# Sharing the last copies of a linear-attention kernel with VectorE, and filling TensorE's waits with products nobody reads

## The chip, the cores and the metric

One core of one Trainium2 chip. The metric is the device time in microseconds (us) of one execution of the whole kernel; each kernel was executed several times, and medians and ranges are given. The profiler's span (first to last instruction, 124.9 us for the kernel before) is some 1.8 us shorter than the time (126.69 us for the same execution).

## The reference, cut to what matters

```python
# Q, K, V: float32 [8, 12, 512, 64]
Q_feat = np.maximum(0, Q); K_feat = np.maximum(0, K)
KV     = einsum('bhkd,bhkv->bhdv', K_feat, V)
K_sum  = sum(K_feat, axis=2)
out    = einsum('bhqd,bhdv->bhqv', Q_feat, KV) / (einsum('bhqd,bhd->bhq', Q_feat, K_sum)[..., None] + 1e-10)
```

96 heads are done in 12 octets of eight. Every byte is read once (37.75 MB) and written once (12.58 MB).

## The kernel before: the parts that matter

An octet (number `o`) passes through these steps: K and V are prepared on VectorE (`prep`), KV is summed on TensorE into one PSUM bank (`mm_kv`), copied to SBUF (`evac_kv`), Q is transposed on TensorE and copied with a ReLU (`qt`), the outputs are made on TensorE and copied (`out_t`), the denominators are made (`denom`), the outputs are transposed back (`back`), divided on VectorE (`norm`) and stored (`store`).

```python
    pou = pool("pou", 2, space=PSUM)            # two buffers, shared by out_t and back
    ps_kv = pkv.tile([P, 2, 256], fp32)         # one PSUM bank for KV
    def evac_kv(o, gs):                         # four copies for half an octet
        for s in range(2):
            for c in range(2):
                nc.scalar.copy(kvd[o % NK][...], ps_kv[64 * s:64 * s + 64, gs, ...])
    def qt(o):                                  # two halves; of the last octet VectorE takes the second
        ...
    def out_t(o):
        for j in range(2):
            ps = pou.tile(..., tag="ps_out")
            ...                                 # 4 products of 256 columns
            copy = nc.vector.tensor_copy if o == NO - 1 and j == 1 else nc.scalar.copy
            copy(ot[o][:, :, 4 * j:4 * j + 4], ps.rearrange(...))
    def store(o, o_sb):
        if o + DELAY < NO:                      # DELAY = 5: hold stores back until later loads have landed
            nc.sync.dma_start(out=scratch, in_=k_sb[2 * (o + DELAY)][0:1, 0, :])
        if o == NO - 1:                         # the last octet in two halves
            for j in range(2): nc.sync.dma_start(out=Ov[:, rs], in_=o_sb[:, rs])
            return
        nc.sync.dma_start(out=Ov, in_=o_sb)     # 1 MB
    def backs(o):
        o_sb = out_tile()
        for j in range(2):
            norm(o, j, back(o, j), o_sb)
        store(o, o_sb)
    ...
    o = NO - 2; g = 2 * NO - 2                  # the last two octets
    ...
    prep(g + 1); prep_v(g + 1, nc.vector)
    backs(o)
    mm_kv(g + 1)
    evac_kv(o + 1, slice(1, 2))
    qt(o + 1)
    out_t(o + 1)
    denom(o + 1)
    backs(o + 1)
```

## Time and profile before

| | before |
|---|---|
| time, first three executions | 126.67 us (126.56 to 126.73) |
| busiest compute engine | PE, 69% of the span |
| HBM traffic over the span | 403 GB/s |
| last normalising round ends | 121.37 us into the span |
| first and second half store issued | 119.88 and 121.40 |
| last mark of the last store, slowest DMA engine | 123.65 |

Two lines of the timeline (start, duration, engine, line and what it does; SPq is SyncE's queue of DMA issues) give the moments at which the last three stores are handed over:

```profile
113.02 0.33 SPq L236 DMA_DIRECT2D out_dram<-o_sb  x1
...
119.88 1.85 SPq L234 DMA_DIRECT2D out_dram<-o_sb  x2
```

The first is the last full store, of octet 10, the second line the two halves of octet 11 (119.88 and 121.40). Here a store that is issued starts only when the DMA engines have done what was issued before it (octet 10's, issued at 113.02, gets its first packets at about 117.0).

### The profile page before, as it was taken

Reading aid. Unit: us, or ns where it says so; the run is one execution under the profiler, and the core shown is the slowest. Engines: PE = TensorE matmul, PEld = TensorE weight load, DVE = VectorE, ACT = ScalarE, POOL = GpSimd, SP = SyncE. Lnnn points to the kernel's source line nnn. Section 1 sums busy time; section 2 is a strip of 40 time slices with the busy share of each in tenths; the row PEclk is TensorE's granted clock in tenths of the full one; section 3 lists DMA queues with packets and bytes.
Section 4 is the critical chain, followed back from the end, with each engine's and each line's share of the span. In section 5 each row is a group of like instructions: output and inputs, shape, how many; then the busy total and the mean of one; then the engine's idle time right before and its main releaser. Section 6 shows DMA issues by size and latency. Waiting matters only on the chain.

```text
span 124.9 us, 2637 instructions
## 1 busy us (share of the span) xinstructions
PE 86.0 (69%) x1056; PEld 78.7 (63%) x1056; DVE 81.6 (65%) x175; ACT 78.9 (63%) x115; POOL 31.3 (25%) x62
## 2 busy tenths in 40 slices
PE   0032297998989899894598596199867757795640
PEld 0041285997878789793597494199756566694630
DVE  2256644749798897979348759532946936994670
ACT  0163369969898998989339589164929928647000
POOL 6902424315253331142133124034022000000000
PEclk9999999999999999999859999657999999999687
DMA  3999999999999999999999999999999999999984
GB/s 102 380 310 214 215 207 210 217 205 214 207 212 211 208 217 326 255 216 297 286 213 284 304 211 252 332 212 234 339 226 217 323 259 216 314 425 420 428 352 197
DMA packets 10748, 32.68 MB, mean 262 GB/s; under 512 B 1392, under 2 KB 1392, under 8 KB 9328
## 3 DMA queue, kind: packets, MB, share of 16 engines
q0 software_dynamic: 8064, 17.83, 74.6%
q1 hardware_dynamic: 2384, 13.63, 27.2%
q10 hardware_dynamic: 288, 1.05, 2.1%
q8 instruction: 8, 0.13, 0.4%
q14 instruction: 4, 0.03, 0.1%
HBM read 37.75 MB, written 12.58 MB: 403 GB/s over the span
## 4 chain that ended last, share of the span: by engine, by line
DMA 34%; PE 28%; DVE 26%; ACT 6%; issue 2%; SPq 0%; DVEq 0%; ACTq 0%; POOLq 0%
DMA v_sb<-in_V_dram 14%; DMA q_sb<-in_Q_dram 13%; DVE o_sb L221 12%; PE ps_kv L148 11%; PE ps_bk L215 8%; DMA kv_first<-in_K_dram 7%; PE ps_qt L171 5%; DVE kf L134 4%; ACT qt L176 4%; PE ps_ot L187 3%; ACT kvd L157 2%; DVE vo L136 2%; DVE vo L143 2%; DVE den L205 1%; DVE rec L209 1%
## 5 line engine op out<-in xcount | busy, mean ns | idle before, releaser
L148 PE MATMUL ps_kv<-vo,kf 128*128 128x132 bf16 x384 | 31.0, 246 | 17.9 <-ACT vo L141 8.2
L148 PEld LDWEIGHTS <-kf 128*128 128x128 bf16 x384 | 28.5, 110 | 19.2 <-DVE vo L136 10.9
L221 DVE TENSOR_TENSOR o_sb<-ps_bk,rec 128x1024 f32<-128x1024 f32 x24 | 28.4, 1220 | 16.7 <-PE ps_bk L215 16.7
L157 ACT CAST kvd<-ps_kv 64x260 bf16<-64x260 f32 (+1 forms) x56 | 19.2, 342 | 18.8 <-PE ps_kv L148 16.1
L176 ACT ACTIVATE qt<-ps_qt 128x1024 bf16<-128x1024 bf16 x23 | 22.4, 1026 | 6.7 <-PE ps_qt L171 6.6
L215 PE MATMUL ps_bk<-ident,ot_sb 128*128 128x128 f32 x192 | 24.5, 284 | 1.1 <-DVE ot_sb L190 1.1
L190 ACT COPY ot_sb<-ps_ot 128x1024 f32<-128x1024 f32 x23 | 23.0, 1013 | 2.9 <-PE ps_ot L187 2.0
L134 DVE TENSOR_SCALAR kf<-k_sb,mask 128x1024 bf16<-128x1024 bf16 x44 | 18.3, 457 | 7.5 <-DMA k_sb<-in_K_dram 7.5
L215 PEld LDWEIGHTS ps_bk<-ident,ot_sb 128*128 128x128 f32 x192 | 22.4, 149 | 1.1 <-ACT ot_sb L190 1.1
L92 POOL DMA_DIRECT2D k_sb<-in_K_dram x22 | 11.9, 542 | 37.9 <-DMA q_sb<-in_Q_dram 20.6
L171 PE MATMUL ps_qt<-ident,q_sb 128*128 128x128 bf16 x192 | 15.2, 243 | 7.2 <-DMA q_sb<-in_Q_dram 7.2
L171 PEld LDWEIGHTS <-q_sb 128*128 128x128 bf16 x192 | 13.7, 110 | 8.2 <-DMA q_sb<-in_Q_dram 8.0
L187 PE MATMUL ps_ot<-qt,kvd 128*128 128x256 bf16 x96 | 14.5, 283 | 5.6 <-DVE o_sb L221 4.3
L94 POOL DMA_DIRECT2D v_sb<-in_V_dram x22 | 12.4, 562 | 17.5 <-DMA k_sb<-in_K_dram 9.5
L187 PEld LDWEIGHTS <-kvd 128*128 128x128 bf16 x96 | 9.3, 100 | 8.2 <-issue 6.1
L136 DVE TENSOR_SCALAR vo<-v_sb,mask 128x1024 bf16<-128x1024 bf16 x22 | 10.7, 488 | 1.5 <-DMA v_sb<-in_V_dram 1.5
L141 ACT ACTIVATE vo<-v_sb,mask 128x1024 bf16<-128x1024 bf16 x10 | 11.5, 1154 | 0.2
L197 PEld LDWEIGHTS <-qt 128*128 128x128 bf16 x192 | 6.8, 97 | 4.4 <-ACT qt L176 3.4
L197 PE MATMUL ps_den<-kvd,qt 128*128 128x16 bf16 x192 | 7.5, 180 | 2.4 <-ACT qt L176 2.1
L98 POOL DMA_DIRECT2D q_sb<-in_Q_dram x12 | 6.5, 544 | 8.2 <-DMA v_sb<-in_V_dram 5.3
L200 DVE SCALAR_TENSOR_TENSOR own<-ps_den,mask_h 128x256 f32<-128x256 f32 x12 | 5.0, 416 | 3.3 <-PE ps_den L197 3.3
L134 DVE TENSOR_SCALAR kf<-kv_first,mask 128x1024 bf16<-128x1024 f32 x4 | 2.8, 751 | 5.1 <-DMA kv_first<-in_K_dram 5.1
(22 smaller groups left out, 26.4 us busy)
## 6 DMA issues: line engine op xcount, KB each, us to landing
out_dram<-o_sb SPq DMA_DIRECT2D x11, 1024.0 KB, 9.1
q_sb<-in_Q_dram POOLq DMA_DIRECT2D x12, 512.0 KB, 14.7
k_sb<-in_K_dram POOLq DMA_DIRECT2D x22, 256.0 KB, 14.1
v_sb<-in_V_dram POOLq DMA_DIRECT2D x22, 256.0 KB, 13.2
kv_first<-in_V_dram ACTq DMA_DIRECT2D x2, 512.0 KB, 7.3
kv_first<-in_K_dram SPq DMA_DIRECT2D x2, 512.0 KB, 6.9
out_dram<-o_sb SPq DMA_DIRECT2D x2, 512.0 KB, 2.7
scratch<-k_sb SPq DMA_DIRECT2D x7, 0.1 KB, 4.8
```

The costliest lines, as they stand in the source:

```text
L94: nc.gpsimd.dma_start(out=v_sb[g].rearrange("p r d -> p (r d)"), in_=Vr[g])
L134: nc.vector.tensor_scalar(kf[g][:, :, s, :], k_sb[g], scalar1=0.0, scalar2=mask[:, 0, s:s + 1], op0=Alu.max, op1=Alu.mult)
L136: nc.vector.tensor_scalar(vo[g % NB][:, :, 0, 2:D + 2], v_sb[g], scalar1=mask[:, 1, 0:1], scalar2=None, op0=Alu.mult)
L148: nc.tensor.matmul(ps_kv[:, g % 2, 0:2 * (D + 2)].rearrange("p (t d) -> p t d", t=2), kf[g][:, r, :, :].rearrange("p s d -> p (s d)"), vo[ ...
L157: nc.scalar.copy(kvd[o % NK][64 * c:64 * c + 64, 4 * gs.start + s:4 * gs.stop:2, c * D1:c * D1 + D1].rearrange("p (g t) d -> p g t d", t=2 ...
L171: nc.tensor.transpose(ps[:, u, :], q_sb[o][:, i * (U // 2) + u, :], ident)
L176: nc.scalar.activation(qt_sb[o % NZ][:, us], ps, Act.Relu)
L187: nc.tensor.matmul(ps[:, i], kvd[o % NK][:, h, 1:2 * D + 1], q[:, :, h, :], start=True, stop=True, skip_group_check=True)
L190: copy(ot[o][:, :, 4 * j:4 * j + 4], ps.rearrange("p h u c -> p u h c"))
L197: nc.tensor.matmul(ps[:, u], qt_sb[o % NZ][:, u, :], kvd[o % NK][:, :, 0:2 * D1:2 * D1 - 1], start=True, stop=True, skip_group_check=True)
L215: nc.tensor.transpose(ps[:, 2 * v:2 * v + 2].rearrange("p c d -> p (c d)"), ot[o][:, 8 * j + v].rearrange("p h c -> p (h c)"), ident32)
L221: nc.vector.tensor_tensor(o_sb[:, rs], ps, rec[o][:, rs].unsqueeze(2).to_broadcast([P, 16, D]), op=Alu.mult)
```

## The change

Its intent: in the last two octets ScalarE does most copies in a row while VectorE waits, and TensorE waits so long for them that its clock is halved. So VectorE takes two of KV's four copies and half of Q ahead of the second normalising round of octet 10, ScalarE takes both output copies of the last octet, and TensorE runs 5 and 6 products into an unread part of a PSUM bank, to look busy to the clock gate.

```diff
+    ps_den = pde.tile([P, 2, 256], fp32, name="ps_den")     # half for denominators, half for idle products
-    def evac_kv(o, gs):
+    def evac_kv(o, gs, share=False):
...
+                copy = nc.vector.tensor_copy if share and c == 1 else nc.scalar.copy
...
+    def idle(n, o):
+        for i in range(n):
+            nc.tensor.matmul(ps_den[:, 1], ident, q_sb[o][:, 2 * i:2 * i + 2, :], start=True, stop=True,
+                             skip_group_check=True)
...
-            copy = nc.vector.tensor_copy if o == NO - 1 and j == 1 else nc.scalar.copy
-            copy(ot[o][:, :, 4 * j:4 * j + 4], ps.rearrange("p h u c -> p u h c"))
+            nc.scalar.copy(ot[o][:, :, 4 * j:4 * j + 4], ps.rearrange("p h u c -> p u h c"))
...
-    backs(o)
+    o_sb = out_tile()
+    norm(o, 0, back(o, 0), o_sb)
+    ps = back(o, 1)
     mm_kv(g + 1)
-    evac_kv(o + 1, slice(1, 2))
-    qt(o + 1)
-    out_t(o + 1)
+    evac_kv(o + 1, slice(1, 2), share=True)
+    for i in range(2):
+        relu_q(o + 1, i, transp(o + 1, i), nc.vector if i == 1 else None)
+    norm(o, 1, ps, o_sb)
+    store(o, o_sb)
+    idle(5, o + 1)
+    out_t(o + 1, (0,))
     denom(o + 1)
+    out_t(o + 1, (1,))
+    idle(6, o + 1)
     backs(o + 1)
```

## The prediction

> **What bounds the kernel now.** I read the 40 slices first, for what is full all the time.
>
> ```profile
> PEclk9999999999999999999859999657999999999687
> DMA  3999999999999999999999999999999999999984
> ```
>
> Each digit is a slice of 3.12 us. The DMA row is 9 from the second slice to the third last: the 16 DMA engines are never short of work, while no compute engine is above 69% of the span. The PEclk row shows the second thing: the granted TensorE clock falls at slices 19 and 25 to 27, and again at the end (6, 8, 7). The change is aimed at that last fall, so the end decides. The second view is the chain that ended last, from 113 us on.
>
> ```profile
> 113.07 1.03 ACT qt L176
> 114.10 0.04 issue
> 114.14 1.05 PE ps_ot L187 x8
> ...
> 115.28 1.23 DVE ot_sb L190
> 116.51 0.14 issue
> 116.65 3.47 PE ps_bk L215 x16
> 120.12 0.02 issue
> 120.14 1.23 DVE o_sb L221
> ```
>
> By it the end is compute: Q's copy, the output products, their copy, 16 transposes in 3.47 us, and the last normalising round, which ends at 121.37. The same 16 transposes took 1.75 us in the same chain at 109.22, so the half clock costs 1.72 us here. But the chain stops at the last instruction and the span ends at 124.9; the rest is the last stores. So third, stretches of the end with DMA share and GB/s as the last two columns (the first figures are the stretch's length and PE, PEld, DVE, ACT and POOL busy, then PEclk).
>
> ```profile
> 108.00:119.00 11.00, 8.50 (x99) 8.20 (x99) 8.24 (x16) 4.98 (x11) 0.00 (x0) 0.88 1.01 418
> 119.00:120.00 1.00, 1.00 (x7) 0.86 (x5) 0.85 (x1) 0.00 (x0) 0.00 (x0) 0.61 0.89 377
> 120.00:121.00 1.00, 0.11 (x1) 0.00 (x0) 0.86 (x1) 0.00 (x0) 0.00 (x0) 1.00 0.64 262
> 121.00:122.00 1.00, 0.00 (x0) 0.00 (x0) 0.37 (x1) 0.00 (x0) 0.00 (x0) 1.00 0.99 406
> 122.00:123.00 1.00, 0.00 (x0) 0.00 (x0) 0.00 (x0) 0.00 (x0) 0.00 (x0) 1.00 0.84 336
> 123.00:124.00 1.00, 0.00 (x0) 0.00 (x0) 0.00 (x0) 0.00 (x0) 0.00 (x0) 0.60 0.50 201
> ```
>
> From 108 to 119 us the DMA engines move 418 GB/s at share 1.01, by then almost only output. What they move is a backlog: the store of the last but one octet is issued at 113.0 and lands 8.4 us later, though 1 MB at 418 GB/s is 2.5 us. The DMA issues say the same (size, then us to landing):
>
> ```profile
> out_dram<-o_sb SPq DMA_DIRECT2D x11, 1024.0 KB, 9.1
> out_dram<-o_sb SPq DMA_DIRECT2D x2, 512.0 KB, 2.7
> ```
>
> So two paths reach the end almost together: compute, whose last half is ready at 121.37, and the store queue. I therefore counted the trace's packets. The five last full stores run back to back from 107.2; their packets finish on the fastest DMA engine at 119.44 and on the slowest at 121.04. That slowest engine took 2.45 us for each of these stores (its marks are 111.22, 113.68, 116.13, 118.58, 121.04), went at once to the first half store (issued 119.88, done there at 122.28) and then to the second (issued 121.40, first packet 122.22, last mark 123.65). It was not idle at all before 122.28.
>
> **What the Trainium skill says.** "TensorE: Matmul & The Clock Gate", Part 1, states a gate on the matmul clock that falls to half after a quiet window of about 3.4 us, the windows running freely. This trace agrees in size: the half-clock stretch runs from 116.37 to 119.78, 3.41 us. Cut on that grid, the windows show how much PE work kept the clock (second figure is PE busy, PEclk is the third last):
>
> ```profile
> 68.58:72.00 3.42, 1.85 (x26) 1.55 (x26) 2.58 (x7) 2.15 (x3) 0.53 (x1) 1.00 1.05 303
> ...
> 75.41:78.82 3.41, 1.68 (x25) 1.16 (x23) 3.34 (x8) 3.16 (x3) 1.06 (x2) 1.00 1.07 278
> 78.82:82.24 3.42, 1.50 (x15) 1.50 (x16) 0.82 (x3) 0.36 (x1) 0.53 (x1) 0.50 1.06 292
> ...
> 112.96:116.37 3.41, 1.45 (x24) 1.35 (x24) 1.74 (x3) 2.12 (x3) 0.00 (x0) 1.00 1.00 418
> 116.37:119.78 3.41, 3.13 (x15) 3.16 (x16) 2.39 (x5) 0.00 (x0) 0.00 (x0) 0.50 1.00 423
> ```
>
> After 1.68 and 1.45 us of PE work in a window the clock fell; after 1.85 it stayed. "PSUM — Partial Sum Buffer", PSUM bank collisions raise a hardware error, says that two engines may not touch one bank and quadrant at once. KV sits in one bank, and in the compiled order VectorE's two copies wait for ScalarE and ScalarE's second for VectorE, so the four copies go in turn; the trace of before, with ScalarE alone, can't show it. "DMA: Bandwidth & Descriptors", Queues, rings and completion order, says that each DMA engine consumes a queue's descriptors in ring order. The trace agrees: stores finish in the order of issue, each about 2.45 us after the one before. The same page, Where 436 GB/s comes from, gives a ceiling of 435 GB/s; 418 measured leaves little.
>
> **The change part by part.** Everything up to 110.6 us is the same: in the compiled order the first 1,725 rows of TensorE do not differ, and no load is moved.
>
> 1. KV's second half. Before: four ScalarE copies, 111.95 to 113.05. Now two of the four are VectorE's. A VectorE pass over 1,024 columns from PSUM took 1.22 us, over 256 columns 0.42, so about 0.29 us (estimate) for 130 columns against ScalarE's 0.27. In turn, with about 0.05 us for each change of engine, that is 1.25 us: ScalarE is done with its part at 112.87, VectorE at 113.2. ScalarE's half of Q starts at 112.9 instead of 113.07: gain 0.17.
> 2. VectorE's half of Q, 0.69 us, now comes before the second normalising round of octet 10: 113.2 to 113.9. So both halves of Q are there at about 113.95, 0.2 earlier than 114.14. That round (1.22) slips from ending at 113.0 to about 115.15, and with it its 1 MB store.
> 3. Output products: the copy of the second half moves from VectorE to ScalarE, which does both in 2 x 1.02 us one after the other: 114.5 to 116.55. Before, the two ran side by side and ended at 116.51. Gain from 1 and 2 given back: the transposes start at about 116.6 against 116.65.
> 4. Denominators: VectorE is free for them from 115.15 instead of 116.42; they were never last.
> 5. Idle products: 5 and 6 of 256 columns. Eight such products took 1.03 us, so about 0.65 and 0.75 us of PE, in gaps where it waits. The window that had 1.45 us of PE work then has some 2.8, over 1.85 by far. I expect the clock to hold whatever the phase of the windows. The 16 transposes then take 1.75 instead of 3.47 us.
>
> Sum for compute: normalising rounds end at about 118.7 and 119.95 instead of 119.86 and 121.37, so the last half is ready 1.4 us earlier. That is 1.1% and would give 125.3 us if nothing stood behind it.
>
> The store queue does. The half stores would be issued at 118.7 and 120.0, but the slowest DMA engine is busy with the full stores to 121.04. It then needs 1.25 us for each half (122.28 less 121.04), so it ends at 121.04 + 2.5 = 123.54 instead of 123.65. Gain: 0.11 us. The faster engines end earlier, which doesn't matter, as a store has landed when its last engine has. The late store of octet 10 costs nothing: it is issued at about 115.2, and even the fastest engine takes up its packets only at about 117.
>
> **The rivals.** (a) Compute alone sets the end: 1.4 us off, 125.3. The chain view speaks for it; the backlog speaks against it. (b) The DMA engines share the end evenly: their idle share from 119 to 123 is 0.11 + 0.36 + 0.01 + 0.16 = 0.64 us, so at most 126.0. Against it: a store's packets are fixed to their engines. But in another execution the spread of 1.6 us may be smaller. (c) The clock falls all the same, or the copies in turn cost more than I think: the last round then ends as before or some 0.3 us later, 126.6 to 127.0. (d) The late store of octet 10 leaves DMA engines idle: it has nearly 2 us of slack, so I give it little.
>
> For the queue speaks also that the three times before lie within 0.17 us. If free-running windows moved the half clock between executions, a compute-bound end would move by up to 1.4 us.
>
> **Range and chances.** The slowest engine gives 126.67 - 0.11 = 126.56; a little weight on (b) brings it to **126.5 us**. Low end 126.0 from (b), high end 126.8 from (c). Over 2% faster needs 124.1, more than the whole compute gain: 0.01. Slower by 2% needs 129.2: 0.01. Within 2%: 0.98.
>
> **What would show it.** Right: PEclk 1.00 up to 120 us and L215's counterpart for the last octet at about 1.75 us; the last normalising round ending near 120.0; DMA share about 1 up to 122 without the dip to 0.64; the half stores' time to landing up from 2.7 to some 3.6 us or more; the last landing moved by 0.1 to 0.6 us only. Wrong: a last landing 1 us earlier (the queue was no bound), a clock that still falls, or KV's four copies at the same time. The prediction fails as a whole if the store backlog at 119 us is smaller, or larger, than in the trace of before.

## The result, and the profile after

The changed kernel took 126.73 us (median of six, 126.59 to 126.78), the kernel before beside it 126.70 (median of six, 126.46 to 127.23; three of the six are those of the table above). The ratio is 0.9996, with a 95% interval from 0.9976 to 1.0016: the same. Here and below a ratio is the mean time of one kernel's fast runs over that of the other's in the same rounds, so not quite the ratio of the medians quoted.

What the change was for did happen. The granted clock and the DMA share by slices, after:

```profile
PEclk9999999999999999999779859959999999999995
DMA  3999999999999999999999999999999999999993
```

The fall of the clock at slices 38 to 40 is gone (only the last slice, with no work left, shows a 5). The chain at the end, after:

```profile
111.24 0.28 ACT kvd L160
111.52 0.02 issue
111.54 0.30 DVE kvd L160
111.84 0.02 issue
111.86 0.28 ACT kvd L160
112.14 0.02 issue
112.17 0.30 DVE kvd L160
...
116.09 1.11 PE ps_bk L228 x8
117.19 0.02 issue
117.22 1.22 DVE o_sb L234
```

KV's copies go in turn between ScalarE and VectorE, as the order of waits had said. Eight transposes now release the first normalising round 1.13 us after they start (117.22 less 116.09), where before it took 1.98 (118.63 less 116.65). The second round ends at 119.57 instead of 121.37. In this execution everything at 110 us was already 0.71 us earlier (octet 10's first round started at 109.93 instead of 110.64), so 1.09 of these 1.80 us belong to the change. Then the stretches of the end, with the columns as in the prediction:

```profile
108.00:119.00 11.00, 8.90 (x108) 7.79 (x105) 8.49 (x16) 4.77 (x10) 0.00 (x0) 1.00 1.01 416
119.00:120.00 1.00, 0.00 (x0) 0.00 (x0) 0.57 (x1) 0.00 (x0) 0.00 (x0) 1.00 1.00 422
120.00:121.00 1.00, 0.00 (x0) 0.00 (x0) 0.00 (x0) 0.00 (x0) 0.00 (x0) 1.00 0.96 397
121.00:122.00 1.00, 0.00 (x0) 0.00 (x0) 0.00 (x0) 0.00 (x0) 0.00 (x0) 1.00 1.03 422
122.00:123.00 1.00, 0.00 (x0) 0.00 (x0) 0.00 (x0) 0.00 (x0) 0.00 (x0) 0.64 0.66 270
123.00:124.00 1.00, 0.00 (x0) 0.00 (x0) 0.00 (x0) 0.00 (x0) 0.00 (x0) 0.50 0.15 61
```

From 120 us on no engine computes any more, and the DMA engines are full up to 122: the dip to 0.64 between 120 and 121 is filled, and what filled it is missing at the end (0.66 and 0.15 instead of 0.84 and 0.50). The half stores wait in the queue, as their time to landing shows, up from 2.7 us:

```profile
out_dram<-o_sb SPq DMA_DIRECT2D x2, 512.0 KB, 4.3
```

Counted by packets, the slowest DMA engine finishes the last half at 123.57 after and 123.65 before. (A mark is the 4-byte packet that ends an engine's share of a store in the trace. The packed trace has no engine numbers; which packets belong to one engine is inferred from their times.) Before, all 16 engines end together, from 123.50 to 123.65, because the fast ones ran out of packets and waited for the hand-overs at 119.88 and 121.40; after, they end one by one from 121.84 on. So the gain of 1.8 us in compute, 1.09 of it by the change, became 0.09 us at the last mark (before rounding), and the spans differ by 0.1 us (124.8 and 124.9). The rest turned into waiting in the store queue.

### The profile page after: what moved, and what is told of

Read it like the earlier page. It is cut to its first block, busy times and chain, and to the rows that moved or that the text cites. A ratio compares the mean times of both kernels' runs of the same rounds, so it can differ in the third digit from the quotient of the medians.

```text
span 124.8 us, 2656 instructions
## 1 busy us (share of the span) xinstructions
PE 86.6 (69%) x1067; PEld 78.5 (63%) x1067; DVE 81.1 (65%) x176; ACT 79.4 (64%) x114; POOL 31.2 (25%) x62
## 4 chain that ended last, share of the span: by engine, by line
DMA 34%; DVE 30%; PE 23%; ACT 5%; issue 2%; DVEq 1%; SPq 0%; POOLq 0%; ACTq 0%
DMA v_sb<-in_V_dram 14%; DVE o_sb L234 13%; DMA q_sb<-in_Q_dram 13%; PE ps_kv L150 11%; DMA kv_first<-in_K_dram 7%; PE ps_bk L228 7%; DVE kf L136 5%; PE ps_qt L171 4%; DVE vo L138 3%; ACT kvd L160 2%; DVE vo L145 2%; PE ps_ot L201 2%; DVE den L218 2%; ACT qt L179 2%; DVE rec L222 1%
## 5 line engine op out<-in xcount | busy, mean ns | idle before, releaser
L160 ACT CAST kvd<-ps_kv 64x260 bf16<-64x260 f32 (+1 forms) x54 | 18.7, 346 | 19.5 <-PE ps_kv L150 16.6
L203 ACT COPY ot_sb<-ps_ot 128x1024 f32<-128x1024 f32 x24 | 24.0, 1014 | 3.0 <-PE ps_ot L201 2.0
L228 PE MATMUL ps_bk<-ident,ot_sb 128*128 128x128 f32 x192 | 23.0, 273 | 0.4 <-ACT ot_sb L203 0.4
L228 PEld LDWEIGHTS ps_bk<-ident,ot_sb 128*128 128x128 f32 x192 | 20.8, 141 | 0.7 <-ACT ot_sb L203 0.7
L171 PE MATMUL ps_qt<-ident,q_sb 128*128 128x128 bf16 x192 | 16.0, 250 | 6.0 <-DMA q_sb<-in_Q_dram 5.9
L171 PEld LDWEIGHTS <-q_sb 128*128 128x128 bf16 x192 | 14.3, 114 | 7.3 <-DMA q_sb<-in_Q_dram 7.1
```

The lines of the kernel that those rows point to most:

```text
L160: copy(kvd[o % NK][64 * c:64 * c + 64, 4 * gs.start + s:4 * gs.stop:2, c * D1:c * D1 + D1].rearrange("p (g t) d -> p g t d", t=2), ps_kv[6 ...
L171: nc.tensor.transpose(ps[:, u, :], q_sb[o][:, i * (U // 2) + u, :], ident)
L203: nc.scalar.copy(ot[o][:, :, 4 * j:4 * j + 4], ps.rearrange("p h u c -> p u h c"))
L228: nc.tensor.transpose(ps[:, 2 * v:2 * v + 2].rearrange("p c d -> p (c d)"), ot[o][:, 8 * j + v].rearrange("p h c -> p (h c)"), ident32)
```

## The experiments

All variants compute the reference's result, except the three that leave out a store, which are marked. "Store queue" is my theory: the slowest DMA engine, never idle, reaches the end of its work at about 123.6 us whatever compute does, as long as compute hands over the last halves in time.

### A queue that is 1 MB shorter, on the kernel before (wrong output on purpose)

```diff
-        nc.sync.dma_start(out=Ov, in_=o_sb)
+        if o != NO - 3:
+            nc.sync.dma_start(out=Ov, in_=o_sb)
```

> The kernel before, without the store of octet 9 (its 1 MB of output stays unwritten: wrong on purpose). Theory (store queue): before, the queue of full stores and the compute tail reach the end within 0.1 us of each other, so with 1 MB (2.45 us of queue) less the compute tail alone sets the end: half stores issued at about 119.9 and 121.4 as now, time 126.3 to 126.7 us, at most 0.4 us less than before. Rival 1 (all bytes count, the DMA engines bound the whole kernel and compute never does): 2.4 us less, 124.3 us.

Measured: 126.09 us median of six, but from 124.34 to 127.06, against 126.76 (126.59 to 127.07, eleven) of before. Three of the six count as slow because they are over 1.5% above the fastest; the fast three are 124.34, 125.04 and 125.91, and give the ratio 0.9867 (0.9825 to 0.9908). That rule cuts off the upper half of a wide spread, so this ratio flatters; the median of all six is 0.5% under before. The expectation (126.3 to 126.7) missed: I had counted on the half clock at the end of every execution. The profiled one (125.91) kept its clock there and had its last round done at 120.27. Its stretches 118 to 120 show the queue run dry:

```profile
118.00:119.00 1.00, 0.73 (x7) 0.49 (x5) 1.00 (x1) 0.00 (x0) 0.00 (x0) 1.00 0.14 57
119.00:120.00 1.00, 0.00 (x0) 0.00 (x0) 1.00 (x2) 0.00 (x0) 0.00 (x0) 1.00 0.03 12
```

What follows: the queue was there; without this megabyte the profiled execution had its last mark at 122.73 instead of 123.65, and there compute set the end. The fastest execution, 2.4 us under before (126.76 less 124.34), is what the rival (all bytes count) had said. It has no trace, so this run alone doesn't exclude the rival. With the queue shortened even the fast executions spread over 1.6 us, while the kernel before spread over 0.5: this suggests that a full queue hides a spread of compute.

### The same on the changed kernel (wrong output on purpose), and once more

> The changed kernel, without the store of octet 9 (wrong on purpose). Theory (store queue): the queue ends on its slowest engine near 118.6 instead of 121.07, so the 1.7 us that the clock saves in the transposes show: last round ends near 119.6 to 119.9, last packet about 2.25 us after the second issue, time 124.9 to 125.3 us, 1.2 to 1.6 us less than the kernel before without this store. Rival 1 (all bytes count): 124.3 us, equal to the kernel before without it. Rival 2 (the earlier compute end is worth nothing in any case, for instance a fixed end of the program): 126.6 us, equal to the kernel before without it.

Measured: 126.46 us (126.02 to 127.06, six), ratio 0.9983 (0.9955 to 1.0011). This missed clearly. In its profile compute and queue were as expected (second half issued at 119.66, 15 of the 16 DMA engines done at 122.08), but one engine ended at 122.91. Among its last packets lies an 8 KB fetch of the queue that the profile calls q14, instruction, at 121.63; two of the 4 KB packets that followed took 368 and 308 ns instead of about 160.

> The changed kernel without the store of octet 9 once more, because its first run missed the 124.9 to 125.3 us expected (126.46). In that run's profile the last halves were done on 15 DMA engines at 122.08 and on one at 122.91, behind an 8 KB instruction fetch of the runtime's queue that began at 121.63 among its packets. Theory (a late fetch on one engine): the profile shows again one engine 0.5 us or more behind the other fifteen with such a fetch among its last packets, and the time is 126.0 to 127.1 us. Rival (chance of that one execution): all sixteen engines end within 0.35 us of each other and the profiled time is 125.0 to 125.4 us.

Measured: 126.49 us (125.95 to 126.87, four), ratio 0.9995 (0.9963 to 1.0027), and the same picture: 15 engines done at 121.92, one at 122.74, with a fetch at 121.46 and again packets of 368 and 308 ns behind it. The DMA share from 121 to 125 us in 40 slices, and that queue's line:

```profile
DMA  8997999400010010000000000000000000000000
...
q14 instruction: 1, 0.01, 0.5%
```

The first eight digits are all engines, the single 1s behind them one engine that is late. "DMA: Bandwidth & Descriptors", Queues, rings and completion order, of the Trainium skill calls row 14 of the queues runtime-internal, refill among its tasks; the traces agree, as the kernel issues nothing on it. The fetch (0.31 us) and the two longer packets (0.21 and 0.15 more than usual) make 0.67 of the 0.8 us by which this engine is late. So without the fetch the two profiled executions would have taken some 125.1 to 125.5 us, an estimate from their times (126.13 and 125.95) less 0.67 to 0.83, near the 124.9 to 125.3 expected. Why the fetch falls between the last packets here, and before them (119.30) in the variant above, no run shows. The slower executions of both runs (126.79 to 127.06) have no trace; that part stays open, and with it why the median hardly moved.

### The copies alone, and the idle products alone

The changed kernel without `idle(5, ...)` and `idle(6, ...)`; and the kernel before with them (the calls alone; `idle` and its `ps_den` as in the change):

```diff
     qt(o + 1)
+    idle(5, o + 1)
     out_t(o + 1)
     denom(o + 1)
+    idle(6, o + 1)
     backs(o + 1)
```

> The changed kernel without its 11 idle products: only the moved copies remain. Theory: the clock falls to half again before the last transposes (16 of them in about 3.4 us instead of 1.75 to 1.97), the last normalising round ends 1.4 to 1.7 us later, near 121.3, and the half stores wait for it; the time stays within 0.2 us of both kernels, 126.6 to 126.9 us, as the queue ends at about the same time. Rival (the copies alone kept the gain, the clock is not what matters): the last round still ends near 119.7 and the clock stays full.

> The kernel before with the 5 and 6 idle products alone, copies as before. Theory: the clock holds, the 16 transposes take 1.75 to 2.0 us, the last normalising round ends near 119.8 as in the changed kernel, because the moved copies give nothing (their gain is given back by ScalarE's two output copies in turn); time 126.5 to 126.8 us, equal to both. Rival (the idle products delay what stands behind them on TensorE, or do not hold the clock): last round at 121.3 or later.

Measured: copies alone 126.86 us (126.67 to 127.36, four), ratio 1.0012 (0.9991 to 1.0033). Idle products alone 126.97 (126.64 to 128.17, four), ratio 1.0032 (0.9995 to 1.0069). Neither differs from before by the interval. The details missed in both, and the second's time its 126.5 to 126.8. In the profiled execution of the copies alone the clock did not fall before the last transposes, so that one execution could not show what the idle products are for. With the idle products alone it did fall, and the last transposes started late. Two lines of the timeline of the idle products alone show why (in brackets, idle time and what ended it):

```profile
115.54 0.41 DVE L206 SCALAR_TENSOR_TENSOR own<-ps_den,mask_h 128x256 f32<-128x256 f32 x1
...
116.01 1.44 PE L183 MATMUL ps_den<-q_sb,ident 128*128 128x256 bf16 x6 [1.30 <-DVE own L206]
```

The six products write the bank that the denominators' pass reads, and in the compiled order they wait for that pass. In the kernel before it stands behind VectorE's output copy (114.40 to 115.63). So products meant to fill a wait stood in front of the transposes until 117.24. In the changed kernel the output copy is ScalarE's and that pass comes at 114.31: the moved copies are what makes room for the second idle products. A variant of it with the six ahead of the denominators tests this (against the diff above):

```diff
     out_t(o + 1)
-    denom(o + 1)
     idle(6, o + 1)
+    denom(o + 1)
     backs(o + 1)
```

> The kernel before with the idle products alone, as in the earlier run, but the second six ahead of the denominators' products instead of behind them. In the earlier run these six waited 1.30 us for the denominators' first VectorE pass, which stands behind VectorE's output copy, and held the transposes up to 117.24. Theory: without that wait the transposes start as the second copy ends (about 4.8 us after the end of Q's transposes, as in before), the clock holds in most executions, time 126.5 to 126.8 us with none above 127.0. Rival (the idle products do not hold the clock without the moved copies): the clock falls in the profiled run and single runs go over 127.0 us.

Measured: 126.68 us (126.56 to 126.91, six), ratio 0.9991 (0.9969 to 1.0013), no execution above 127.0, and in the profile eight transposes in 1.08 us from 116.81, with the clock at full. One profile can't show that the idle products hold the clock: it also held in those of the copies alone and of the shortened queue on the kernel before, which have none. The mean granted clock for every execution says more. The profiles in which it fell under the last transposes have a mean of 0.929 to 0.938, those in which it held 0.940 or more. In all 46 executions with idle products that wait for nobody (the changed kernel, its variants with these products, and this one) the mean is 0.938 or more; under 0.938 are 31 of 40 executions of before and two of the four of the copies alone. This kernel's six, without any moved copy, have 0.941 to 0.952. So the idle products hold the clock, in most executions at least, where they wait for nobody; and again the time is the same.

### More work in front of the last stores

The first normalising round of the last octet is done again, once or three times, with the same values:

```diff
-            norm(o, j, back(o, j), o_sb)
+            ps = back(o, j)
+            norm(o, j, ps, o_sb)
+            if o == NO - 1 and j == 0:
+                for _ in range(1):        # or 3
+                    norm(o, j, ps, o_sb)
```

> The changed kernel with the first normalising round of the last octet done twice (the same values again, 1.22 us more of VectorE ahead of both half stores; results stay right). Theory (store queue): the halves were issued at 118.5 and 119.6, and the slowest DMA engine would take them up only at 121.07 and 122.3, so both have about 1.8 us to spare: time 126.6 to 126.8 us, within 0.15 us of the changed kernel. Rival (the last round sets the end): 1.2 us more, 127.9 us.

> The same with three more rounds, 3.66 us of VectorE ahead of both half stores. Theory: 1.8 us of it fall into the slack and the rest shows, 1.7 to 2.1 us more than the changed kernel, 128.4 to 128.8 us. Rival (the last round sets the end): 3.7 us more, 130.4 us. If the queue had more slack than the packets say: less than 1.5 us more.

> The kernel before with one more such round. Theory: here compute and queue ended within 0.1 us of each other where the clock had fallen, so in executions with the half clock at the end the 1.22 us show (127.7 to 128.0 us), in executions whose clock held they show in part or not at all; median of 127.0 to 127.9 us, clearly more than the changed kernel with the same round. Rival (both kernels end by the queue with the same slack): within 0.15 us of before.

| kernel | VectorE work added | time, us | ratio to before |
|---|---|---|---|
| changed, one round more | 1.22 us | 126.88 (126.54 to 127.16) | 1.0003 (0.9978 to 1.0028) |
| changed, three more | 3.66 us | 128.77 (128.70 to 129.11) | 1.0156 (1.0131 to 1.0181) |
| before, one more | 1.22 us | 127.09 (126.69 to 127.90) | 1.0030 (0.9997 to 1.0062) |

This is the clearest answer. 1.22 us straight in front of the last stores cost the changed kernel nothing that the interval (0.25%, 0.3 us) resolves; of 3.66 us, 2.0 show (128.77 less 126.73) and 1.6 were free. Where they show, the DMA engines are idle; the stretches 120 to 122 of the changed kernel with three rounds more:

```profile
120.00:121.00 1.00, 0.00 (x0) 0.00 (x0) 0.97 (x2) 0.00 (x0) 0.00 (x0) 1.00 0.37 156
121.00:122.00 1.00, 0.00 (x0) 0.00 (x0) 1.00 (x1) 0.00 (x0) 0.00 (x0) 1.00 0.00 0
```

The median with one round more lies just above the 126.6 to 126.8 expected, and two of its six executions took 127.15 and 127.16. The second has the trace, and there compute did set the end: KV's copies came 0.85 us later than in the first profile of the changed kernel (a half-clock window from 100.11 to 103.52 went before; that it is the cause is not shown), the halves were handed over at 120.57 and 121.70, and the DMA engines ran short in the same stretches:

```profile
120.00:121.00 1.00, 0.00 (x0) 0.00 (x0) 1.00 (x2) 0.00 (x0) 0.00 (x0) 1.00 0.39 164
121.00:122.00 1.00, 0.00 (x0) 0.00 (x0) 0.67 (x1) 0.00 (x0) 0.00 (x0) 1.00 0.63 254
```

The first half came 2.1 us later than in that profile and the last mark 0.55 (124.12 less 123.57): again some 1.5 us were free. So the slack is real but not wide: a start that is 0.85 us late and one round more together use it up.

The kernel before with one more round is less decided than I expected: 0.3% over before, with an interval that just touches 1. Two of its six executions lie at 127.64 and 127.90, four at 127.16 or less. The profiled one (126.86) had its tail at half clock but had started it early, the last transposes at 115.79 against 116.65 in the first profile of before.

### The changed kernel again, and the stores held back one octet more

```diff
-    DELAY = 5
+    DELAY = 6
```

> The changed kernel again, unaltered, to see more executions beside the kernel before on one chip. Theory: the store queue sets its end in every execution, so its times stay between 126.5 and 126.9 us whatever the mean granted clock, while those executions of before whose mean clock is under 0.93 lie 0.2 to 0.5 us above those over 0.93; in the mean the changed kernel is 0 to 0.3 us faster, ratio 0.9975 to 1.0005. Rival (no execution of before is bound by compute): the two means within 0.05 us and no relation to the clock.

> The kernel before with its stores held back one octet more (one number, and one output buffer more). Theory: loads come before 1 MB more of stores, so the compute tail may end up to 2.4 us earlier against a store queue that ends where it did; then the queue covers the tail even at half clock, without any of the change: 126.4 to 126.8 us, no execution above 126.9. Rival (the bytes do not move, or the last loads are bound by their buffers): as before, with executions above 127.0.

> The changed kernel with the same one number altered. Theory: the queue already sets its end, so more slack for compute is worth nothing: within 0.15 us of the changed kernel, 126.5 to 126.8 us. Rival (compute still sets part of the end): 0.3 us or more faster than the changed kernel.

Measured: the changed kernel again 126.77 us (126.59 to 127.54, six), ratio 1.0006 (0.9984 to 1.0027); before held back 126.69 (126.67 to 126.87, five), ratio 0.9992 (0.9979 to 1.0005); changed and held back 126.75 (126.46 to 126.80, six), ratio 0.9990 (0.9975 to 1.0004).

Held back one octet more, loads go ahead of 1 MB more of stores and compute ends far earlier. In the changed kernel the first normalising round of the last octet is the one below, the last half is handed over at about 116.9 us instead of 119.6, and lands 7.1 us after its issue:

```profile
114.56 1.22 DVE o_sb L234
```

```profile
out_dram<-o_sb SPq DMA_DIRECT2D x2, 512.0 KB, 7.1
```

The span of that execution is 125.0 us. Compute ends 2.7 us earlier than in the changed kernel and the time doesn't move: nothing on the compute side sets this end. The kernel before, held back, has the half clock under its last transposes (16 in 3.42 us from 113.75) and yet its five times lie within 0.2 us, 126.67 to 126.87: one number takes the compute tail off the end as the whole change does.

The repeat of the changed kernel missed its expectation in two executions, 127.02 and 127.54. The first has the trace: TensorE had a half-clock window from 100.34 to 103.75, the last rounds came 1.0 us later than in the first profile, and again one engine met a fetch (122.76) with packets of 368 and 308 ns behind it and ended at 123.87, 0.21 us after the next one. The relation of before's times to its mean clock, which I expected, shows in the rounds of the added normalising work (six executions under 0.93: 126.91 to 127.28; five above: 126.45 to 126.76) but not here (four under 0.93 at 126.65, 126.72, 126.97 and 127.14; seven above, 126.56 to 126.95). It stays open. No variant was clearly faster than both kernels.

## Why the prediction was right

- **The end is set by the store queue**: right. 123.54 was predicted for the slowest engine's last mark, 123.57 measured; this close because the backlog was the same in both executions (the slowest engine ended the full stores at 121.04 and 121.07). Shown by the added rounds (1.6 us free) and by the held-back stores (2.7 us earlier, same time).
- **KV's copies in turn, 1.25 us**: right, 1.23 (111.24 to 112.47), with 0.30 us for VectorE's against 0.29 estimated. The rule that the prediction cites, by bank and quadrant, explains only a part: the second and third copy read different partitions (0 to 63, 64 to 127) of the bank. That the third waits for the second is the compiled order; copies at the same time were not tried.
- **Idle products hold the clock, 0.65 and 0.75 us**: right, 0.71 and 0.82 us, and the mean clocks above bear it out; variants show that their place matters, which the prediction did not see: it took them to lie in gaps only, and with the old copies the second six lengthen the path.
- **Transposes start 0.05 us earlier, compute ends 1.4 us earlier**: mis-sized. Counted from octet 10's first round, the transposes start 0.15 us later (6.16 against 6.01 us), and compute ends 1.09 us earlier. One wait was missed: the second output products need a PSUM buffer that octet 10's second normalising round still holds. TensorE's line says so:

```profile
114.37 0.33 PEld L201 LDWEIGHTS <-kvd 128*128 128x128 bf16 x4 [0.21 <-DVE o_sb L234]
```

  It cost little, as ScalarE was still at the first output copy (113.94 to 114.96). Most of the late start was in plain sight: the prediction has the first output copy 0.55 us after its products start (113.95 to 114.5), where before's trace has 0.69 (114.14 to 114.83) and after's 0.70. The other error is the transposes: 1.75 us was the piece of them that the chain shows, while the timeline of before has octet 10's 16 at full clock in 1.91 us (from 109.05), and after took 1.97. The first release came after 1.13 us, not the 0.9 that the sum has.
- **A misread row**: counted from 1, as in "second slice", the earlier falls of the clock are in slices 20 and 21 and 26 to 28, not 19 and 25 to 27. Nothing rests on it.
- **The late store of octet 10 costs nothing**: right. Issued at 114.34 instead of 113.02, and the DMA share stays at 1.01 from 108 to 119.
- **The even end (rival b) and compute alone (rival a)**: neither came. Idle DMA time moved from before the last half to after it.
- **"The three times before lie within 0.17 us"** was weak support: 43 more executions of before spread from 126.45 to 127.28. The conclusion stood on the packets, not on it.
- **The gain of 0.11 us** itself is below what the timing resolves (interval of 0.4%); only the profiled pair, 0.09 us at the last mark, speaks for it.

## What to carry to other kernels

When the DMA engines are full up to the last microseconds, follow the last store's packets back instead of the last instruction's chain: time saved in front of a store that waits in a queue is only waiting time. A cheap test is to add work in front of the last store; what is free there is what a speed-up there cannot earn; look at more than one execution, as the free time differs with what happened earlier. And filler work must wait for nothing: products meant to keep a clock up cost time where a buffer makes them wait in front of real ones.

## What the Trainium skill lacked or had wrong

- "TensorE: Matmul & The Clock Gate", Why this matters for your kernels, advises against idle gaps over some 3 us. Here the clock fell after a window whose longest gap was 1.33 us (112.81 to 114.14); PE was busy for 1.45 of its 3.41 us. The page tells of a clock that swings with short idle times too, but gives no amount of work that holds it. In this trace 1.45 and 1.68 us were followed by a fall and 1.85 was not, but there is no clean threshold: in other traces 1.51 us (shortened queue, from 117.22) and 1.61 (the same on the changed kernel, from 78.40) were followed by full clock, and 1.76 (idle products alone, from 112.16) by a fall.
- The same page does not say that filler products can hold the clock through such a tail: 11 products, 1.5 us of PE work, go with a mean clock of 0.938 or more in 46 of 46 executions, against 9 of 40 of before.
- "DMA: Bandwidth & Descriptors" does not say how far the 16 engines drift apart (it calls two of them usually slower, without a figure for it; these traces have no engine numbers): after five stores back to back they finished between 119.44 and 121.04 us, 1.6 us apart, and the slowest set the end.
- The same page names row 14 but not what a fetch on it costs among the last packets: in both traces of one kernel an 8 KB instruction fetch there went with one engine ending 0.8 us behind the other fifteen.
